# Eight transfers instead of one for the store of one output tile of an attention-like einsum

## The chip, the cores and the metric

The kernel runs on one core of a Trainium2 chip. The metric is device time in microseconds (us) of that core. Besides the time there is a profile of one execution; its span is some 1.8 us shorter than the time of the same execution.

## The reference

```python
def setup_inputs():
    batch, n_heads, seq_t, seq_s, channels = 8, 12, 512, 512, 64
    return {"x": randn(batch, n_heads, seq_t, channels), "y": randn(batch, n_heads, seq_s, channels)}  # float32

def reference(x, y):
    return np.einsum('bhtc,bhsc->bhts', x, y).astype(np.float32)
```

25.2 MB are read and 100.7 MB are written, so the output is what has to move.

## The kernel before

The output is made in 48 tiles of 128 rows of 16 KiB (2 MiB each). A tile is written into one of five slots, which input loads use as well. Each tile is stored by one transfer from the SyncE queue. The parts that matter:

```python
    Q = P // G                      # 16
    ...
    K = 8
    E = R // K                      # 4
    SLOTS = 5
    ...
    ov = out.rearrange("b h t s -> (b h t s)").rearrange(
        "(o u h q n) -> o h q u n", u=2, h=2, q=Q * E, n=K * S
    )                               # a tile: 64 x 2 rows of 4096 float32
    ...
    slots = ctx.enter_context(tc.tile_pool(name="slots", bufs=SLOTS))
    ...
    def result(o):
        i, h = divmod(o, 2)
        xT, yT = made[i]
        otf = slot()
        ot = otf.rearrange("p (r s) -> p r s", s=S)
        for k in range(0, K, 2):
            pm = pmpool.tile([P, 2, S], fp32)
            ...                     # two matmuls into pm
            if k == 4:
                nc.vector.tensor_copy(ot[:, k:k + 2, :], pm)
            else:
                nc.scalar.activation(ot[:, k:k + 2, :], pm, COPY)
        ...                         # work for later tiles
        return lambda: nc.sync.dma_start(ov[i, h], otf)
    ...
        for store in stores:
            store()
        for o in range(len(stores), 4 * NG):
            result(o)()
```

## Time and profile before

| | before |
|---|---|
| time, median of 3 | 302.47 us (302.41 to 302.53) |
| span in the profile | 300.8 us |
| busy: PE, VectorE, ScalarE, GpSimd | 45%, 63%, 67%, 27% |
| packets of the store and load queue | 98.6% of 16 DMA engines' span |
| moved over the span | 418 GB/s |

No compute engine is near its limit, and the DMA engines have no free time: the transfers bound this kernel. A line of a timeline is: start us, duration us, engine, line of the kernel, operation, output<-input, count. "SPq" is the queue from which SyncE issues transfers. A line of waits is: who waited <- for whom, us in total, times, longest us.

For tile 25 and its neighbours the waits of the issue queue before, from 165 to 200 us, are these two:

```profile
SPq L145 <- DVE slot L138: 19.3, 7, 2.8
SPq L145 <- ACT slot L140: 12.9, 8, 1.6
```

The queue waits only for the copies that fill a slot, not for a transfer.

Much of what follows rests on one more source, the landing events in the trace. Each full-width transfer gives 16 of them, one per DMA engine. I write "first" and "last landing" of a store for the earliest and the latest of its 16, and "spread" for the time between them. The "late engine" is the one that lands last, the "leaders" are those that land first. (No view of the profile prints these events one by one; they, and the single packets told of below, were read from the packed trace.) Before, store 25 (counting from 0) has first 188.76 and last 191.73; the last store, 47, has first 296.19 and last 299.94. One engine is late, and the run ends with it.

### The profile page before, as it was taken

The page shows a single profiled execution, that of the slowest core. Times are in us where ns is not written, and L with a number is a line of the kernel's source. Part 1 is how long each engine was busy: PE and PEld are TensorE (multiplying, and loading weights), DVE is VectorE, ACT ScalarE, POOL GpSimd, SP SyncE. Part 2 cuts the span into 40 slices and gives each one's busy share as a digit, 9 for nine tenths or more (in the row PEclk, how much of TensorE's full clock was granted, in tenths as well). Part 3 has the DMA queues.
Part 4 walks back from the last instruction along what each step waited for, and adds up shares of the span by engine and source line. Part 5 has one row for each costly group of instructions (what it writes and reads, how often), then busy time and mean ns, then how long its engine had stood idle before and what let it go on. Part 6 is the DMA issues. An engine that isn't in the chain of part 4 may idle for free.

```text
span 300.8 us, 1489 instructions
## 1 busy us (share of the span) xinstructions
PE 136.8 (45%) x377; PEld 46.9 (16%) x384; DVE 189.4 (63%) x157; ACT 201.1 (67%) x187; POOL 82.0 (27%) x59
## 2 busy tenths in 40 slices
PE   0004044317554546555647654748554657552000
PEld 0001011102221212121212121212121212210000
DVE  1568998896997668665767587667765675313000
ACT  4666598998986867686668676777677664647000
POOL 1899989991211011101110111011100100000000
PEclk9999575677999777785775689765679865779555
DMA  7999999999999999999999999999999999999994
GB/s 281 433 421 421 422 426 422 421 442 427 419 444 418 427 440 421 442 429 423 443 421 427 442 418 438 431 423 440 426 426 440 425 431 431 421 421 447 423 423 172
DMA packets 10377, 125.93 MB, mean 419 GB/s; under 512 B 1152, under 2 KB 1152, under 8 KB 1152
## 3 DMA queue, kind: packets, MB, share of 16 engines
q1 hardware_dynamic: 10368, 125.83, 98.6%
q8 instruction: 3, 0.05, 0.1%
q14 instruction: 6, 0.05, 0.0%
HBM read 25.17 MB, written 100.66 MB: 418 GB/s over the span
## 4 chain that ended last, share of the span: by engine, by line
DMA 66%; DVE 13%; ACT 10%; issue 2%; PE 1%; ACTq 0%; SPq 0%; DVEq 0%
DMA out_dram<-slot 57%; DMA slot<-in_y_dram 9%; ACT slot L140 8%; DVE yb L67 5%; DVE xT L115 3%; DVE slot L138 2%; ACT xk L82 1%; DVE yT L120 1%; PE pm L134 1%; ACT yb L65 1%; DVE xb L67 0%; ACTq L193 0%; SPq L74 0%; DVEq L138 0%; ACTq L140 0%
## 5 line engine op out<-in xcount | busy, mean ns | idle before, releaser
L134 PE MATMUL pm<-yT,xT 128*128 128x512 bf16 x377 | 136.8, 513 | 137.5 <-ACT slot L140 100.8
L140 ACT ACTIVATE slot<-pm 128x1024 f32<-128x1024 f32 x144 | 136.9, 1025 | 63.2 <-DMA out_dram<-slot 58.5
L138 DVE COPY slot<-pm 128x1024 f32<-128x1024 f32 x48 | 58.8, 1224 | 71.9 <-DMA out_dram<-slot 67.1
L67 POOL COPY xb<-xk 32x1024 bf16<-32x1024 bf16 x42 | 62.2, 1481 | 145.5 <-DVE xT L115 144.4
L134 PEld LDWEIGHTS <-xT 128*128 128x128 bf16 x384 | 46.9, 122 | 226.9 <-issue 190.8
L115 DVE STREAM_TRANSPOSE xT<-xb 128x1024 uint32<-128x1024 uint32 x24 | 49.4, 2060 | 0.7
L67 DVE CAST yb<-slot 64x1024 bf16<-64x1024 f32 x24 | 35.2, 1468 | 13.5 <-DMA slot<-in_y_dram 13.2
L82 ACT ACTIVATE xk<-slot 128x2048 bf16<-128x2048 f32 x12 | 22.9, 1910 | 9.6 <-DMA slot<-in_x_dram 9.5
L67 DVE COPY xb<-xk 32x1024 bf16<-32x1024 bf16 x36 | 26.3, 732 | 0.5
L120 DVE STREAM_TRANSPOSE yT<-yb 128x512 uint32<-128x512 uint32 x24 | 25.0, 1041 | 0.0
L65 ACT ACTIVATE xb<-xk 32x1024 bf16<-32x1024 bf16 x18 | 24.0, 1336 | 0.4
L67 POOL CAST yb<-slot 64x1024 bf16<-64x1024 f32 x12 | 18.9, 1572 | 8.0 <-DMA slot<-in_y_dram 7.3
L65 ACT ACTIVATE yb<-slot 64x1024 bf16<-64x1024 f32 x12 | 15.9, 1326 | 3.5 <-DMA slot<-in_y_dram 3.4
L82 ACT ACT_TABLE_LOAD x1 | 1.3, 1283 | 0.7 <-PEq L182 0.7
L150 DVE MEMSET xb<- 128x1024 uint32 x1 | 0.9, 912 | 1.0 <-PEq L182 1.0
L151 POOL MEMSET xb<- 128x1024 uint32 x1 | 1.0, 952 | 0.3 <-POOLq L182 0.3
L182 POOL MEMSET const-float32-0.0<- 128x1 f32 x1 | 0.1, 98 | 0.2 <-issue 0.2
L182 POOL MEMSET const-float32-1.0<- 128x1 f32 x1 | 0.1, 98 | 0.0
L182 POOL MEMSET const-bfloat16-1.0<- 128x1 bf16 x1 | 0.1, 98 | 0.0
L182 POOL MEMSET const-uint8-127<- 128x1 uint8 x1 | 0.1, 98 | 0.0
## 6 DMA issues: line engine op xcount, KB each, us to landing
out_dram<-slot SPq DMA_DIRECT2D x48, 2048.0 KB, 21.7
slot<-in_x_dram SPq DMA_DIRECT2D x12, 1024.0 KB, 17.5
slot<-in_y_dram SPq DMA_DIRECT2D x12, 1024.0 KB, 19.3
```

The lines of the kernel that those rows point to most:

```text
L65: nc.scalar.activation(dst, src, COPY)
L67: engine.tensor_copy(dst, src)
L82: nc.scalar.activation(xk.rearrange("p r c -> p (r c)"), both[:, :R * C], COPY)
L115: nc.vector.transpose(xT.rearrange("p (k r e) -> p k e r", k=K, e=E), xb.rearrange("p (k e c) -> p k e c", k=K, e=E),)
L120: nc.vector.transpose(yT.rearrange("p (r j) -> p j r", r=D), yb.rearrange("p (j c) -> p j c", c=D))
L134: nc.tensor.matmul(pm[:, two, :], xT[:, k + two, h, :], yT[:, h * S:(h + 1) * S], start=True, stop=True)
L138: nc.vector.tensor_copy(ot[:, k:k + 2, :], pm)
L140: nc.scalar.activation(ot[:, k:k + 2, :], pm, COPY)
L150: nc.vector.memset(zeroed[0], 0.0)
L151: nc.gpsimd.memset(zeroed[1], 0.0)
L182: nc = _bacc.Bacc("TRN2", target_bir_lowering=False, num_devices=1)
```

## The change

For tile 25 of 48, three quarters of each row go out by one transfer over all 128 rows. The last quarter of each row goes out by one transfer over 96 rows and by two each over 7, 5 and 4 rows. The intent is not stated in the source. The name says "uneven", and the bytes and the arithmetic stay the same. One transfer becomes eight.

```diff
+    UNEVEN = 2 * NG + 1
 ...
-        return lambda: nc.sync.dma_start(ov[i, h], otf)
+        if o != UNEVEN:
+            return lambda: nc.sync.dma_start(ov[i, h], otf)
+
+        def store():
+
+            most, n = 3 * K * S // 4, Q * E
+            nc.sync.dma_start(ov[i, h][:, :, :most], otf[:, :most])
+            nc.sync.dma_start(ov[i, h][:48, :, most:], otf[:96, most:])
+            for u in range(2):
+                for lo, hi in ((48, 55), (55, 60), (60, 64)):
+                    nc.sync.dma_start(ov[i, h][lo:hi, u, most:], otf[2 * lo + u:2 * hi + u - 1:2, most:])
+
+        return store
```

## The prediction

> **What bounds the kernel now.** I read the page's slices first, then its queue line, then the chain of work that ended last.
>
> The slices and the queue, from the page of the kernel before:
>
> ```profile
> DMA  7999999999999999999999999999999999999994
> ...
> q1 hardware_dynamic: 10368, 125.83, 98.6%
> ```
>
> The digits are the mean busy share of the 16 DMA engines in each fortieth of the span: 9 or more everywhere but at the ends. The queue's packets fill 98.6% of 16 engines' time. Against that, section 1 has ScalarE at 67% and VectorE at 63%. So transfers are the bound, and 125.8 MB have to move whatever the stores look like. The chain, late in the run (start us, length us, what):
>
> ```profile
> 179.91 21.70 DMA out_dram<-slot
> 201.62 0.02 issue
> 201.64 0.02 ACTq L140
> 201.65 0.04 issue
> 201.70 2.87 ACT slot L140 x3
> 204.56 0.02 issue
> 204.58 21.73 DMA out_dram<-slot
> ```
>
> A store takes 21.7 us from issue to landing; its slot is then refilled in 2.9 us and stored again. One tile has 2 MiB and a store lands every 4.9 us, so 21.7 us is a queue of 4.4 stores, not slowness of one. With five slots, four stores are always queued.
>
> One thing the page doesn't show comes from the landing events in the trace (the 16 increments of each store's completion semaphore, one per DMA engine). For store 24 the first engine lands at 183.89 us and the last at 186.82, so one engine is 2.9 us behind; at the last store it is 296.19 and 299.94. Eleven or so engines stay within 0.7 us of the first in the middle stores. The span, 300.8, ends right after the slowest engine. **So the end is set by one late engine, and the others have up to 3.8 us to spare.** From landing to landing the leader needs 4.87 us a store (86.69 to 261.87 in 36 stores), the laggard 4.95 (87.74 to 265.76).
>
> **How many transfers may be open.** The second fact that the prediction rests on is in the first microseconds of the issue queue's timeline (start us, length us):
>
> ```profile
> 4.29 0.49 SPq L75 DMA_DIRECT2D slot<-in_y_dram  x1
> 5.63 0.33 SPq L74 DMA_DIRECT2D slot<-in_x_dram  x1
> 8.07 0.33 SPq L75 DMA_DIRECT2D slot<-in_y_dram  x1
> ```
>
> and in the waits of that queue in the first 9 us (us in total, times, longest):
>
> ```profile
> SPq L75 <- DMA slot<-in_y_dram: 2.1, 1, 2.1
> SPq L74 <- DMA slot<-in_x_dram: 0.8, 1, 0.8
> ```
>
> Eight loads go out back to back, the ninth stops. It fills the fifth slot, which nobody has used, so it waits for no buffer. It waits for the first load, which landed at 5.61 us; the tenth waits for the second, landed at 8.05. The trace has eight completion semaphores that take turns, each with 144 increments, which is nine transfers of sixteen. **A transfer is therefore not issued until the transfer eight places before it has landed.** The stores of the kernel before never feel this, as five slots hold at most five open stores. A tile stored by eight transfers will.
>
> **What the Trainium skill says.** "DMA: Bandwidth & Descriptors", section "Why a DMA increments its semaphore by 16 and not by 1": a transfer runs on the largest k up to 16 that divides the slowest dimension of both of its patterns, on the lowest-numbered k engines. The page of before agrees for k = 16: 1152 packets under 512 B are 16 for each of 72 transfers. No trace of before has another k. The same page, "Anatomy of one DMA": engines don't wait on semaphores, the issuing sequencer does; this fits the stop at 5.63. Its "Latency and other measured facts" gives about 600 ns to the first byte; here the first issue ends at 1.13 us, the engines' first packets start between 1.76 and 2.41, so 0.63 to 1.28 us.
>
> **The change part by part.** The tile is store 25 (counting from 0), transfer 49 with the 24 loads. It is issued here, with the next four tiles:
>
> ```profile
> 170.04 0.54 SPq L145 DMA_DIRECT2D out_dram<-slot  x1
> 174.95 0.54 SPq L145 DMA_DIRECT2D out_dram<-slot  x1
> 179.91 0.54 SPq L145 DMA_DIRECT2D out_dram<-slot  x1
> 184.81 0.54 SPq L145 DMA_DIRECT2D out_dram<-slot  x1
> 189.81 0.54 SPq L145 DMA_DIRECT2D out_dram<-slot  x1
> ```
>
> (1) Bytes: the same. One transfer becomes eight: 12 KiB from all 128 rows, 4 KiB from 96 rows, then 7, 5 and 4 rows of 4 KiB twice.
>
> (2) Issue: seven more at about 0.54 us are 3.8 us of the issue queue. It is idle nearly all of its 4.9 us a store, and engines have some 20 us queued. By itself worth nothing.
>
> (3) Packets: a 16 KiB packet takes 611 ns and follows the one before by 607; an 8 KiB one takes 309. Smaller packets thus cost a few ns each, and a completion packet 9 ns. With some ten packets more per engine: below 0.1 us.
>
> (4) Uneven engines: by the skill's rule 64 rows and 96 rows go over 16 engines (120 KiB each); 7, 5 and 4 rows over engines 0-6, 0-4 and 0-3. Engines 0-3 get 6 rows (144 KiB instead of 128), engine 4 gets 136, 5 and 6 get 128, 7-15 get 120. At 0.607 us per 16 KiB: +0.61 us on engines 0-3, +0.30 on 4, -0.30 on 7-15. Only the late engine's share counts, and which one it is I can't tell.
>
> (5) The rule of eight: parts 1 to 8 wait for transfers 41 to 48. By 170.04, 41 to 44 have landed, so four parts go at once. The fifth waits for 45 (171.99), the sixth for 46 (176.93), the seventh for 47 (181.85), the eighth for 48, store 24, at 186.82. Until then the queue stands still, and stores 26 to 28, ready at 174.95 to 184.81, stand behind it. Store 26 must then wait for part 1: the late engine starts that when it is done with store 24, at about 186.4 (its data ends 0.45 us ahead of a landing: 299.49 against 299.94), and takes 8 x 0.457 = 3.66 us: data done at 190.0, landed at about 190.5. Then 0.54 of issue and 0.63 to 1.28 to the first packets: **store 26 starts moving at 191.7 to 192.3.** The late engine has part 2 left meanwhile (6 x 0.155 = 0.93 us, to 191.0), so it is idle for 0.7 to 1.3 us (less the 0.6 if it is one of 0-3, whose extra rows fill just this gap). The leaders, 2.9 us ahead, are idle for some 3.5 us, from about 188.5.
> In the kernel before the late engine began store 26 at 191.28 (store 25 landed at 191.73). So it starts **0.4 to 1.0 us later**, and the imbalance of (4) disappears in the gap. Stores 27 to 29 wait for parts 2 to 4, landed by then, and are ready: four stores are queued at once, steady state is back.
>
> (6) Something comes back. After the gap all engines start store 26 together, without the 2.9 us lag. 22 stores are left. The late engine needed 108.2 us for them (191.73 to 299.94), 4.92 each; at 4.86, its pace between 88 and 142 us, where the spread stayed at 1.0 to 1.7, it would be 107.0. At most 1.2 us is won; instruction fetches and whatever slows this engine will start over, so I count 0.4.
>
> Sum: 302.47 + 0.7 (start later) + 0.1 (packets) - 0.4 = about 302.8 us.
>
> **Rivals.** A: *imbalance alone.* No stall at the issue queue, the late engine gets +0.61, +0.30 or -0.30: 302.2 to 303.1. For it: the queue is deep. Against it: the stop at 5.63. B: *hidden entirely*, as the bytes are the same and most engines have 3 us to spare: 302.4 to 302.6. The stop in (5) speaks against it for the leaders, but their spare time is just what absorbs theirs. C: *the small parts fall on one engine* (k = 1 for all six: 32 rows, 128 KiB): that engine gets 4.9 us more, less the 0.3; if it is a leader, 3 us are hidden and 1.5 to 2 show, otherwise 4.6: 304 to 307. The skill's rule gives 7, 5 and 4 instead, so I find this unlikely. D: *the stall is worse*: the stores behind it wait for each part in turn, each with its own 2 us of issue and landing: two or three such rounds make 306 to 308. Against it: parts 3 to 8 are tiny and land with part 2.
>
> **Range and chances.** Step (5) has a width of 0.6 us, step (6) of 1.2; together they reach from 302.0 to 303.6, and a little more upward for C and D: 301.9 to 303.8. 2% would be 6.0 us: slower needs D or the worst of C, 3%; faster by 6 us has no mechanism, 1%.
>
> **What would show it right or wrong.** Right: the last part is issued at about 186.8, store 26 at about 190.5 instead of 174.95, a dip of the DMA share at 188 to 192, then stores 26 to 29 within some 2 us; the spread of landings near zero afterwards. The six small parts have 7, 5 and 4 completion packets. Step (5) falls if stores 26 to 28 go out at their old times; (6) falls if the spread is back at 3 us within a few stores. The prediction would be wrong if the gap drained the whole queue more than once, or if slot refills, which wait for all eight parts, came late by more than the queue holds.

## The result, and the profile after

The changed kernel took 304.27 us (median of 3; 304.18 to 304.76) against 302.47, some 1.8 us more. The ratio is 1.0065, 95% interval 1.0046 to 1.0085. (A ratio is the mean time of one kernel's runs over that of the other's in the same rounds, so not quite the ratio of the medians.) The time lies above the predicted range of 301.9 to 303.8. The profiled execution is the slowest of the three, 304.76 us, with a span of 303.0.

From the page of the changed kernel, the slices and the queue:

```profile
DMA  7999999999999999999999999799999999999995
...
q1 hardware_dynamic: 10544, 125.83, 98.1%
```

Where every slice but the first and last was at 9, one is now at 7: slice 26, from 189 to 197 us. The issue queue's timeline shows what lies ahead of it (the part issued at 173.79 is left out):

```profile
169.16 0.54 SPq L152 DMA_DIRECT2D out_dram<-slot  x1
170.07 1.03 SPq L153 DMA_DIRECT2D out_dram<-slot  x1
171.15 1.40 SPq L156 DMA_DIRECT2D out_dram<-slot  x1
172.62 1.13 SPq L156 DMA_DIRECT2D out_dram<-slot  x1
...
176.97 0.73 SPq L156 DMA_DIRECT2D out_dram<-slot  x1
181.92 0.70 SPq L156 DMA_DIRECT2D out_dram<-slot  x1
186.85 0.62 SPq L156 DMA_DIRECT2D out_dram<-slot  x1
190.70 0.62 SPq L147 DMA_DIRECT2D out_dram<-slot  x1
191.68 0.58 SPq L147 DMA_DIRECT2D out_dram<-slot  x1
```

L152, L153 and L156 are the eight parts, L147 is store 26 and those behind it. The last three parts go out at the moments at which stores 22, 23 and 24 land, and store 26 at 190.70, where it went out at 174.95 before. The waits of the queue from 165 to 200 us, after:

```profile
SPq L156 <- DMA out_dram<-slot: 10.4, 3, 4.2
SPq L147 <- ACT slot L141: 3.6, 4, 1.6
SPq L147 <- DMA out_dram<-slot: 3.4, 2, 3.2
```

Transfers now wait for transfers: 10.4 us in three of the small parts, 3.4 us in the stores behind. Nothing of the kind was there in this stretch before. The chain that ended last (start us, us, what) passes through this place:

```profile
170.07 21.53 DMA out_dram<-slot
191.61 0.02 issue
191.62 0.03 SPq L147
191.65 0.03 issue
191.68 10.77 DMA out_dram<-slot
```

Store 27, issued at 191.68, waited for part 2 of tile 25. It lands 10.77 us after its issue instead of 21.7: the queue of stores in front of it had drained.

What the drained queue did is seen in a table of one stretch. The line has the stretch, its length, then the busy time of PE, weight loads, VectorE, ScalarE and GpSimd, and at the end the granted clock, the share of the DMA engines and GB/s. Before:

```profile
188.00:192.00 4.00, 3.40 (x8) 1.15 (x8) 1.69 (x4) 3.30 (x4) 0.00 (x0) 0.57 0.98 418
```

After:

```profile
188.00:192.00 4.00, 2.10 (x8) 0.77 (x8) 1.53 (x3) 3.12 (x3) 0.00 (x0) 1.00 0.30 120
```

For these 4 us the DMA engines worked at 0.30 of their time. And yet the late engine lost little there. Store 26 landed last at 197.52 instead of 196.67, **0.85 us later**. The last store landed at 302.05 instead of 299.94, **2.11 us later**. So 1.26 us of the loss in this trace arise after store 26, where the two programs issue the same stores.

The transfers' list on the page of after has the parts one by one:

```profile
out_dram<-slot SPq DMA_DIRECT2D x1, 1536.0 KB, 21.5
out_dram<-slot SPq DMA_DIRECT2D x1, 384.0 KB, 21.5
out_dram<-slot SPq DMA_DIRECT2D x2, 28.0 KB
out_dram<-slot SPq DMA_DIRECT2D x2, 20.0 KB
out_dram<-slot SPq DMA_DIRECT2D x2, 16.0 KB
```

The time to landing is blank for the small parts, since their semaphore had 8, 6 and 5 events instead of 16. That is 7, 5 and 4 engines and one event at the issue. It agrees with the Trainium skill ("DMA: Bandwidth & Descriptors", "Why a DMA increments its semaphore by 16 and not by 1"), by which the issuing sequencer writes the missing count itself: the first event of a small part comes 1.0 to 1.8 us after its issue, and data would have had to wait for the stores ahead.

Theories for the 1.26 us at this point. **S**: the stall costs a gap and then leaves all engines at a slower pace. **U**: the uneven rows or the small transfers bring the slow pace. **P**: my step 6, which said that the restart wins time back. Later comes **H**: the gap takes away the other engines' lead over the late one, so that a later delay of another engine, hidden before, reaches the end.

### The profile page after: what moved, and what is told of

The parts are those of the page before. It is cut to its first block, busy times and chain, and to the rows that moved or that the text cites. A ratio compares the mean times of both kernels' runs of the same rounds, so it can differ in the third digit from the quotient of the medians.

```text
span 303.0 us, 1510 instructions
## 1 busy us (share of the span) xinstructions
PE 138.2 (46%) x384; PEld 46.8 (15%) x384; DVE 189.4 (63%) x157; ACT 201.1 (66%) x187; POOL 82.0 (27%) x59
## 4 chain that ended last, share of the span: by engine, by line
DMA 68%; ACT 11%; DVE 9%; issue 2%; PE 1%; ACTq 0%; SPq 0%; DVEq 0%
DMA out_dram<-slot 60%; ACT slot L141 9%; DMA slot<-in_y_dram 9%; DVE yb L68 5%; DVE xT L116 2%; ACT xk L83 1%; PE pm L135 1%; DVE slot L139 1%; DVE yT L121 1%; ACT yb L66 1%; ACTq L206 0%; ACT xb L66 0%; SPq L75 0%; ACTq L141 0%; DVEq L139 0%
## 5 line engine op out<-in xcount | busy, mean ns | idle before, releaser
L135 PE MATMUL pm<-yT,xT 128*128 128x512 bf16 x384 | 138.2, 513 | 138.8 <-ACT slot L141 104.0
```

The costliest lines, as they stand in the source:

```text
L135: nc.tensor.matmul(pm[:, two, :], xT[:, k + two, h, :], yT[:, h * S:(h + 1) * S], start=True, stop=True)
```

## The experiments

All have the reference's results. The median of the kernel before on the chip of these runs was 302.51 to 302.53 us. Diffs are against the changed kernel unless they say otherwise.

**e1_gap_only: the stall without parts.** Against the kernel before: tile 25 is stored whole, and behind it in the queue is a 512-byte load into the same slot, which must wait for that store to land.

```diff
+        def store():
+            nc.sync.dma_start(ov[i, h], otf)
+            nc.sync.dma_start(otf[:1, :128], xv[0][:1, :128])
```

> Tile 25 is stored whole by one transfer, and behind it the issue queue has one small load into the same slot, so it must wait until store 25 has landed: a stall of the queue with no uneven rows and no small stores. Theory S (the stall costs twice: a gap, and after it a slower pace of all engines, 4.98 us a store at the late engine instead of 4.92): store 26 is issued at about 192.3 instead of 174.95 and lands at about 199.1; more than 40 per cent of the 16 KiB packets after 200 us are at 614 ns or longer (before: 5 per cent until 240 us); time about 302.47 + 2.45 + 1.25 = 306.2, at least 305.5. Rival U (the slow pace comes of the uneven rows or the small transfers): the share of long packets stays near 5 per cent, and the time is 302.47 + 2.45 = 304.9 or less. Rival P (my prediction, step 6: the restart in step wins time back): below 304.5.

Measured: 306.01 us, ratio 1.0114 (1.0098 to 1.0129). Store 26 was issued at 192.12 and landed last at 198.86, 2.19 us later than before. The last store landed at 303.39, 3.45 us later, so 1.26 us again arose after store 26. The gap in the table of stretches:

```profile
188.00:192.00 4.00, 3.29 (x8) 1.05 (x8) 1.45 (x3) 3.07 (x3) 0.00 (x0) 0.57 0.17 70
```

P falls, and so does U for this run: a gap is enough for the 1.26 us, and no uneven rows are needed.

**e2_even_eight: eight parts, all over 16 engines.**

```diff
-            for u in range(2):
-                for lo, hi in ((48, 55), (55, 60), (60, 64)):
-                    nc.sync.dma_start(ov[i, h][lo:hi, u, most:], otf[2 * lo + u:2 * hi + u - 1:2, most:])
+            cut = (0, 176, 344, 520, 688, 856, 1024)
+            for lo, hi in zip(cut, cut[1:]):
+                nc.sync.dma_start(ov[i, h][48:, :, most + lo:most + hi], otf[96:, most + lo:most + hi])
```

> Eight transfers as in the change, but the last 32 rows go out in six pieces of columns, each over all 16 engines: the same stall, no uneven engines. Theory S: as the changed kernel within 0.4 us, 303.9 to 304.7 (ratio 1.005 to 1.0075), store 26 issued at about 190.6, long packets above 40 per cent afterwards. Rival U: about 303.3, the 0.85 us of the gap alone, and few long packets.

Measured: 304.55 us, ratio 1.0067 (1.0054 to 1.008), as the change. Its stretch:

```profile
188.00:192.00 4.00, 2.69 (x8) 0.80 (x7) 1.35 (x2) 2.96 (x3) 0.00 (x0) 0.59 0.45 169
```

Eight parts are enough; 7, 5 and 4 rows are not needed.

**e3_uneven_five: the same uneven rows in five parts.**

```diff
-            for u in range(2):
-                for lo, hi in ((48, 55), (55, 60), (60, 64)):
-                    nc.sync.dma_start(ov[i, h][lo:hi, u, most:], otf[2 * lo + u:2 * hi + u - 1:2, most:])
+            for lo, hi in ((48, 55), (55, 60), (60, 64)):
+                nc.sync.dma_start(ov[i, h][lo:hi, :, most:], otf[2 * lo:2 * hi, most:])
```

> The same rows on the same engines as in the change (7, 5 and 4 row pairs, so engines 0 to 3 get 144 KiB, 7 to 15 get 120), but five transfers instead of eight, so that the wait for the transfer eight places before ends long before the queue runs dry: uneven engines, no gap. Theory S: 302.2 to 303.1 (ratio 0.999 to 1.002), no dip of the DMA share at 188 to 192 us, 5 per cent long packets until 240 us. Rival U: 303.5 or more, with many long packets after 190 us.

Measured: 303.47 us, ratio 1.003 (1.0017 to 1.0043). The time was above what S expected by 0.4 us and just below what U expected. There was no gap:

```profile
188.00:192.00 4.00, 3.28 (x8) 1.03 (x7) 1.34 (x2) 2.96 (x3) 0.00 (x0) 0.62 1.06 406
```

Here the imbalance shows by itself. From store 24 to store 26 the late engine needed 10.41 us of landings (186.65 to 197.06) instead of 9.85. The last landing moves on by 0.33 us with the 7-row part and by 0.32 with the 5-row part, but the 4-row part landed earlier than either. So the late engine takes part in the first two and not in the third. If the lowest-numbered engines are used, as the skill's section has it, it is engine 4; no run shows engine numbers. From store 26 on the late engine kept its old pace (197.06 to 300.33, 4.918 us a store, as before). But the other engines were slow without any gap: 39 to 45% of the 16 KiB packets between 200 and 240 us took 614 ns or longer ("long packets"; the usual time is 611), against 4 to 6% before. The slow pace of the leaders therefore does not need a gap, and it cost nothing here. S in its first form, "slow pace costs time", is in doubt.

**e4_two_tiles: the change at stores 25 and 35.** Two lines: `UNEVEN = (2 * NG + 1, 2 * NG + 11)` and `o not in UNEVEN`.

> The change at stores 25 and 35. Theory S: the second stall costs its gap again, some 0.85 us, but the slow pace is there already: 304.27 + 0.85 = 305.1 (304.7 to 305.6). If each such tile costs the whole 1.8 us: 306.1. If the second costs nothing: 304.3.

Measured: 306.00 us (305.63 to 306.46), ratio 1.0116. The number that I expected was missed by 0.9 us: the second tile cost about as much as the first. In its trace the late engine at store 35 is another one. All six small parts move its last landing on by 0.17 to 0.19 us each, and the 96-row part by 1.9 us instead of 1.0, and it landed at 243.66 us. The store behind was issued at 240.75, so by an estimate from the first packets of the run (0.6 to 1.3 us after an issue's end) the others restarted at about 242, while this engine was still at its parts. Here the uneven rows did fall on the engine that counts.

**e7_four_cols: small packets, even engines, no stall.** Tile 25 in four transfers of 4 KiB from each of 128 rows.

```diff
+            for lo in range(0, K * S, 1024):
+                nc.sync.dma_start(ov[i, h][:, :, lo:lo + 1024], otf[:, lo:lo + 1024])
```

> Tile 25 goes out in four transfers of 4 KiB from each of the 128 rows: all engines even, no more than four transfers, so no long wait at the issue queue. It asks what brings the slow pace in the run with five uneven transfers, which had no gap. If small packets alone do: over 35 per cent of the packets at 614 ns or longer between 200 and 240 us, the leaders at 4.91 us a store. If it takes uneven engines or a gap: 5 per cent, the leaders at 4.87. Time by either: 302.5 plus the longer way of the small packets, 302.6 to 302.9.

Measured: 302.79 us, ratio 1.0006 (0.9994 to 1.0019). The share of long packets stayed at 4% until 210 us, was 21% in the ten us after that, and 39 to 50% from 220 us on; instruction-fetch packets (the trace marks some packets, on two queues of their own, as "instruction") stand at 216.1 and 221.3 us. In the kernel before it rises in the same way from some 247 us on, with no change at all (17% between 240 and 250 us, 37 to 41% later). So leaders slip into the slow pace after several sorts of disturbance, and while another engine is late it costs nothing.

**e5_early and e6_late: the change at store 5, and at store 40.** One line each: `UNEVEN = 5`, `UNEVEN = 40`.

> The change at store 5 instead of 25; the gap falls at some 95 us. Theory H (what costs beyond the gap is that the gap takes away the other engines' lead, so that later hits on them, at the instruction fetches of about 174, 216 and 254 us, reach the end): this early the late engine is only 1 us behind, its own later hits are still to come, and it builds up its lag again: about +0.85 us, 303.2 to 303.6. Theory R (every restart leaves all engines at the slow pace, 4.91 us a store, for the rest of the run): 41 stores at 4.91 after a first landing near 98.6 us end at 299.9, with 1.7 us of the hit at 254 on top: +1.7, 304.0 to 304.5. The share of 16 KiB packets at 614 ns or longer between 110 and 240 us is 5 per cent by H, over 40 by R.

> The change at store 40; the gap falls at some 265 us, after the last instruction fetch (254 us). Theory H: only the gap is left to cost, +0.85 us: 303.2 to 303.6, and the spread of the last landings is below 0.5 us (before: 3.8). Rival W (each such tile costs 1.8 us wherever it stands, as the second one of the two-tile run did): 304.3.

Measured: 303.57 us at store 5 (ratio 1.0032), 303.70 at store 40 (1.0037). Both are as H had it or 0.1 above, and W falls. R was right about the pace at store 5: 47 to 60% long packets from 90 us to the end, and 4.909 us a store. But its time came out too high, because I had put the first landing after the gap at 98.6 instead of 97.91 us. H's number at store 5 is in part luck: it expected 5% long packets and a late engine that builds up its lag again, and neither came (the spread stayed at 0.3 to 1.2 us until the fetch at 176 us). So e5 alone does not decide between H and R; it takes the next pair.

**e9_at36 and e10_at38: two places, two stores apart.** `UNEVEN = 36` puts the gap just ahead of the instruction fetch at some 254 us, `UNEVEN = 38` puts it over that fetch.

> The change at store 36: the gap falls at some 243 to 247 us, just ahead of the last instruction fetch (254 us). Theory H (the gap takes away the lead, so a later hit on another engine reaches the end): store 37 lands last at about 251.9 instead of 250.97, all engines within 0.5 us; the hit at 254 then puts one engine about 2.1 us behind, and with ten stores at 4.91 the last landing is at 302.5 to 302.8: +2.5 to +2.8 us, 305.0 to 305.4, the worst place of all. Rival R (only a slow pace counts, it grows with the stores that are left): between the cost at 25 (+1.8) and at 40 (+1.1), 303.6 to 304.1.

> The change at store 38: the gap falls at some 253 to 258 us, while or after the last instruction fetch hits. Theory H: the engine hit at 254 has its loss made up while all wait for the late one, as at store 40: +0.9 to +1.2 us, 303.4 to 303.8, the last store's landings within 0.7 us. Rival R: as at 36, 303.6 to 304.1. Two stores apart the two places should differ by over 1 us by H.

Measured: **304.88 us at store 36** (304.31 to 304.91, ratio 1.0075, 1.0063 to 1.0088) **and 303.35 at store 38** (303.22 to 303.88, ratio 1.0031, 1.0018 to 1.0044). Fewer stores are left after 36 than after 25, and yet it costs more; R's 303.6 to 304.1 for both is out. H's 305.0 to 305.4 at 36 is missed by 0.1 us at the median and its 303.4 to 303.8 at 38 by 0.05, and the step of over 1 us is there: 1.5 us. The gaps of e9:

```profile
240.00:244.00 4.00, 2.18 (x6) 0.71 (x5) 2.93 (x2) 3.17 (x4) 0.00 (x0) 0.50 0.64 222
244.00:248.00 4.00, 1.68 (x4) 0.46 (x3) 2.28 (x3) 1.06 (x2) 0.00 (x0) 0.50 0.53 219
```

and of e10, where 6 to 8 of the 16 engines are at work while the fetch passes (252.63 to 253.51 us):

```profile
252.00:256.00 4.00, 1.89 (x7) 0.77 (x8) 3.14 (x3) 1.86 (x3) 0.00 (x0) 1.00 0.31 104
```

The hit itself is visible in the packets. These are all packets of 16 KiB between 248 and 262 us that took over 650 ns in e9 (start and end us; q8 is the instruction queue, q1 the stores):

```
253.14-253.97 q1   253.97-254.94 q1   254.93-255.86 q8   255.84-256.86 q1
```

Each starts within 0.02 us of the end of the one before, so I take them for packets of one DMA engine; the trace has no engine numbers. Three store packets and one fetch take 3.7 us, where three store packets alone take 1.8. That engine comes out 1.9 us behind, and the spread of landings jumps from 0.30 at store 37 to 2.11 at store 38. Before, the same pattern stands at 252.54 to 256.27 us, and there it strikes an engine that is ahead: the last landing goes on by 4.9 us a store, as if nothing had been.

The same accounts for every run with one gap, from the landing events (us; "gap" is how much later than before the first store behind the gap has its last landing, "after it" is what was added by the end):

| | gap | after it | last store: first, last landing | time, median |
|---|---|---|---|---|
| before | | | 296.19, 299.94 | 302.47 |
| change at store 5 | 0.45 | 0.53 | 299.18, 300.92 | 303.57 |
| change at store 25 | 0.85 | 1.26 | 300.38, 302.05 | 304.27 |
| e2, eight even parts at 25 | 0.64 | 1.18 | 300.17, 301.76 | 304.55 |
| e1, gap only at 25 | 2.19 | 1.26 | 301.74, 303.39 | 306.01 |
| change at store 36 | 0.86 | 1.38 | 300.62, 302.18 | 304.88 |
| change at store 38 | 0.71 | 0.09 | 300.53, 300.74 | 303.35 |
| change at store 40 | 0.98 | 0.11 | 300.84, 301.03 | 303.70 |

With the gap behind the last fetch all engines finish within 0.21 us, and only the gap is paid. With the gap ahead of it, one engine finishes 1.6 to 1.8 us behind the first, and that is paid too.

**e11_pool_small: the small parts from GpSimd's queue.** `nc.gpsimd.dma_start` in place of `nc.sync.dma_start` for the six small parts. They then use six other semaphores.

> The change at store 25, but its six small parts are issued from GpSimd, which has completion semaphores of its own; the stores' queue then has two parts of the tile only and never waits for the transfer eight places before. If the wait is what makes the gap: store 26 is issued near 174.95, no dip at 188 to 192 us, 302.4 to 303.5 like the run with five uneven transfers. If the small transfers themselves make it: 304 or more.

Measured: 303.62 us (303.11 to 303.66), ratio 1.0033 (1.0021 to 1.0046), 0.1 above the range but with the stall gone. Store 26 was issued at 174.49, and the stretch has no gap:

```profile
188.00:192.00 4.00, 2.10 (x8) 0.77 (x8) 1.89 (x4) 3.50 (x5) 0.00 (x0) 1.00 1.02 385
```

So the wait for the transfer eight places before made the gap, not the small transfers. On that queue the small parts also moved at once, from 174.1 to 182.2 us, and did not stand behind the earlier stores; e3, which keeps their order, has no gap either. What is left of the cost is about that of e3. In the profiled execution, the fastest of the five (303.11 us), the last store landed at 299.97, only 0.03 us later than before; the other 0.5 us came after the last landing (1.34 us to the end of the span, before 0.84). Why is not shown.

**e8_relief and e12_relief_last: unevenness turned to use** (against the kernel before). If one engine sets the end, bytes could be moved off it. Half of the row goes from all rows, the rest from 96 rows over 16 engines and from 32 rows in four transfers over the four engines that seemed to have time to spare; at store 40, and at store 47.

```diff
+            most = K * S // 2
+            nc.sync.dma_start(ov[i, h][:, :, :most], otf[:, :most])
+            nc.sync.dma_start(ov[i, h][:48, :, most:], otf[:96, most:])
+            for lo in range(48, 64, 4):
+                nc.sync.dma_start(ov[i, h][lo:lo + 4, :, most:], otf[2 * lo:2 * lo + 8, most:])
```

> Uneven on purpose, at store 40 and in six transfers: half the row from all rows, then the second half of 96 rows over 16 engines and of the other 32 rows in four transfers on engines 0 to 3 alone. Engines 0 to 3 get 176 KiB instead of 128, all others 112. In the run with five uneven transfers the last landing moved on by two rows with the 7 and the 5 row parts and not with the 4 row part, so I take the late engine for engine 4. If so: 16 KiB less is -0.6 us, smaller packets +0.2 to 0.3, so 302.0 to 302.3, faster than the kernel before by 0.2 to 0.5 us. If the late engine is one of 0 to 3: +1.8 us, 304.3.

> The uneven store in six transfers that moves 16 KiB off all engines but 0 to 3, now at the last store, where nothing runs behind it that the transfers over few engines could disturb but the late engine's own packets. If the late engine is engine 4 and is left alone: -0.6 us, smaller packets +0.2: 301.9 to 302.3. If the transfers on engines 0 to 3 hold it up as at store 40, where 8 KiB packets took 600 to 1200 ns instead of 309: 303 or more.

Measured: 305.61 us (ratio 1.0105) and 304.26 (ratio 1.006). Both miss the gain that I hoped for. In e8 the engines are busy and move less:

```profile
262.00:266.00 4.00, 3.51 (x8) 1.10 (x8) 0.07 (x1) 1.72 (x2) 0.00 (x0) 0.50 1.01 340
```

Before, that stretch had a share of 1.05 at 446 GB/s. In e8 many 8 KiB packets took 600 to 1213 ns, which otherwise take 309, and 16 KiB packets up to 1247. The late engine needed 3.64 us of landings for its part of the 96 rows (263.65 to 267.29), for 48 KiB, which are 1.9 us at the usual pace. In e12 it needed 3.27 us instead of 2.49 for the half row (295.04 to 298.31). Yet it is no longer the engine that lands last. In e8 the four engines landed their last small part at 267.05, 267.65, 268.28 and 268.95, and the full store behind shows landings 4.86 us after each, the last at 273.81; the late engine's, from 267.29, is that at 272.22. In e12 it was done at 300.15, 0.21 us later than before, and the last small part landed at 301.45. So the end was set by one of the four engines that took the bytes: by 1.6 us over the late engine in e8, by 1.3 in e12. In e8 the lengthened packets begin at 258.8 us, and no engine had landed its share of the 96 rows before 261.80. So the four-row transfers, which come behind it on each engine, did not begin them: the transfer over 96 rows is enough. The runs show transfers slowed while one over fewer than 128 rows runs beside them. The skill ("DMA: Bandwidth & Descriptors", "The descriptor swizzle") has each engine of a 128-partition transfer on an SBUF port of its own; other row counts would mix engines and ports. That would explain it, but it is argued, not shown: the trace has no ports. It fits that in e3 16 of the 128 4 KiB packets took over 200 ns, and of the 512 in e7, which all come from 128-row transfers, none did.

No version tried beats the kernel before.

## Why the prediction was right or wrong

**What bounds the kernel** was read right: in every run the end followed the last landing of all by 0.8 to 1.4 us (before: 300.8 against 299.94).

**Steps (1) to (3)**, bytes, issue and packets, were right in kind and small. The even four-part run puts the price of small packets at 0.12 us on the late engine for a whole tile (5.03 instead of 4.91 us of landings between stores 24 and 25), where I had below 0.1. One detail was off: issues that follow close on one another took 1.03 to 1.40 us instead of 0.54, over few engines or over all 16 (the full stores issued at 192.37 and 193.81 took 1.34 and 1.32), and those of small parts after a wait 0.62 to 0.73. The stall hid this.

**Step (4)**, uneven engines, was right. The k of 7, 5 and 4 show in the events, and the imbalance was hidden in the gap, as e2 with even parts costs as much. Without the gap (e3) it shows.

**Step (5)**, the rule of eight, was right to a few tenths. The eighth part was expected at 186.8 and came at 186.85, store 26 at 190.5 and came at 190.70. Store 26 was to be 0.4 to 1.0 us late on the late engine and landed 0.85 late. e11, which takes the parts out of the rule, removes the stall. Rival D, one stall after the other, did not come.

**Step (6) is the step that failed**: "Something comes back ... I count 0.4". Two terms were mis-sized.
- The pace. I had all engines go at 4.86 us a store after the restart, and called that the late engine's pace between 88 and 142 us. This was misread: its landings there, 87.74 and 141.83 over 11 stores, give 4.92; 4.86 is the leaders' pace (86.69 to 140.13). Only without the fetch at 95 us does the late engine come to 4.87 (98.00 to 141.83). Measured from store 26 to store 47, the first landings went from 197.27 to 300.38, 4.910 a store over 21 stores, nearly the late engine's 4.918 before. Won: 0.17 us instead of up to 1.2.
- The hits to come. I wrote that "instruction fetches and whatever slows this engine will start over", but let them only shrink the gain, from 1.2 to 0.4; I counted no loss for hits on other engines. The leaders' lead of some 3 us had been hiding those. After the restart the spread was 0.25 us. It rose to 1.38 at store 30, with the fetch at 217 us, and had shrunk to 0.68 when the fetch at 255 us put one engine 2.2 us behind. 1.67 us of that were left at the end: 1.67 - 0.25 = 1.42 lost. My own sign of a wrong step (6), the spread coming back, was there.

Together 0.85 - 0.17 + 1.42 = 2.10 us, against 2.11 in the trace. This is the same trace taken apart, no second test; the test of the hits is the pair e9 and e10. The trace is of the slowest of the three runs; the medians differ by 1.8. The sum of the prediction had 0.7 + 0.1 - 0.4, which makes 302.87 and not 302.8. The lead left out of account also explains why the range was too narrow: the range was built around the late engine alone, as if that engine were bound to stay the late one.

Rivals A and B are out by e1 and e2, where even engines cost as much or more, and B by the result itself. C is out by the events of 7, 5 and 4.

**What stays open.** Why the leaders go at 4.86 us a store for most of the run before, and at 4.91 once they have been disturbed, is not settled. The share of packets of 614 ns or longer goes from 5% to some 50%, with a gap (e1), without one (e3), and in the undisturbed kernel after 247 us. That the hits come with the fetches is shown by the fetch packets' place between lengthened store packets and by the pair e9 and e10. How a fetch lengthens the packets beside it is not: two of them run before its own packet starts (253.14 to 254.94 us in e9), and in e10 no 16 KiB store packet near the fetch took over 650 ns. Which instruction stream they belong to was not looked into.

## What to carry to other kernels

Where one late engine sets the end, the time that the others have to spare is not free: it hides their own later delays, and a stall in which all wait for the late one spends it. So the price of a stall is the gap plus what the lost lead would still have hidden, and this depends on what comes after. When a store is cut into parts, count how many transfers may be open on a queue; in this build it was eight, and the parts of one tile used them all up.

## What the Trainium skill lacked or had wrong

- "DMA: Bandwidth & Descriptors" has the choice of k and the sequencer's own write right (8, 6 and 5 events for parts of 7, 5 and 4 rows). It gives no price on this chip for an issue over fewer than 16 engines: 0.62 to 0.73 us of the issue queue after a wait, against 0.55 for the 16-engine parts of e2. Nor does it say that issues close behind one another take 1.0 to 1.8 us even over 16 engines (the change, e2).
- The same page advises against splitting a transfer in halves because they share all engines. It lacks that transfers over fewer rows can slow those beside them: 8 KiB packets of 600 to 1213 ns instead of 309 and full-width 16 KiB packets of up to 1247 instead of 611 (e8), at 340 GB/s with the engines' share at 1.01.
- "Runtime: NRT & Kernel Launch" ("Instruction fetch mechanics") has fetches in blocks of 16 KiB and calls their cost mostly hidden. It gives no price for the DMA engine that carries one, and it was hidden only where that engine had time to spare (store 36 cost 1.5 us more than store 38): the 16 KiB fetch and the three store packets around it took 0.83 to 1.02 us each instead of 0.61, and that engine came out about 1.9 us behind.
- "DMA: Bandwidth & Descriptors" ("Latency and other measured facts") has engines 7 and 15 as usually slower and ties this to transfers issued from GpSimd. Here, with SyncE's transfers, one engine drifts 3.8 us behind over 240 us, so that the end belongs to one of sixteen. By the page's own rule of the lowest-numbered engines it is neither 7 nor 15: it took part in the parts of 7 and 5 rows and not in that of 4 (e3).
